# VectorE in the source's order in the experts' loop, with the gathered rows inside it; gates in column strips; the rows of f - m by way of DRAM; two weight loads ahead of the turn

## The chip, the cores and the metric

The kernel runs on one core of a Trainium2 chip. The metric is the device time of one execution in microseconds (us); smaller is better.

## The reference, cut to what matters

One decoder layer for 512 tokens (and 16 learned ones in front) of width 1024, in fp32. A diagonal state-space branch (S5) and a matrix-memory branch (mLSTM, four heads) are mixed by sigmoid gates; then each token picks 8 x 16 of 16384 single-neuron experts by product keys:

```python
y_s = s5_branch(u_s, ...) @ w_ssm_out          # ends in gelu, and a glu with w_glu
y_m = mlstm_branch(x_m, z_m, ...) @ w_ml_out
mixed = sigmoid(g_s) * y_s + sigmoid(g_m) * y_m
h = h + mixed @ w_out
...
gates = concatenate([q, k, v]) @ w_if + b_if   # mLSTM: log_i and log_f of each head
...
act = gelu(einsum('td,thkd->thk', xb, u_tab[eidx]))
out = einsum('thk,thkd->td', gate * act, v_tab[eidx])
```

## The kernel before, in words

`front` computes the branches and the mix, `peer` the experts. Products that need more than the fast fp32r format gives are done in three matmuls on a high and a low half (`mm3`, `proj`); `split` makes the halves: ScalarE copies the high half (L78), VectorE or GpSimd subtracts (L79). `wblock` (L156) loads a weight block through SP and splits it; two raw blocks and two pairs of halves exist at a time.

**Order.** The source is not the order of execution: a scheduler gives each engine and each queue its order from an estimated timeline, and the hardware then follows that order, each engine by itself. `keep_in_program_order` pins instructions of one engine against each other in the source's order; `later` and `after` only tell the scheduler that one thing comes after another.

**The turn (L560 to L583).** The S5 output ys lies with time in the partitions. Eight DMAs write it to yd in DRAM and eight read it back as yt, channels in the partitions, SP and ScalarE in turn. gsgate(4) and (5) stand behind it in the source, gsgate(6) and (7) after the gates (L650); gelu of yt, glu and so (w_ssm_out) follow.

**The gates (L550 to L605).** log_i and log_f of four heads, from xct and xmt (8 blocks of 128 channels each): each block is split, and the split weights wgt (100 columns wide, high and low halves in strips of their own) times high and low part give 64 matmuls into two accumulators. VectorE and ScalarE add up the strips into li and xf, and xf is transposed (xtp) for the log-sigmoid.

**Decay weights (L796).** `weights(h)` spreads head h's row of f - m (amu) over 128 partitions by a matmul with a selector (sel), then fourteen exponentials on ScalarE fill pm. It runs one head ahead of its use, at the top of the loop over heads.

**The experts' loop (L1401).** The first 128 tokens' experts are fetched row by row: `fetch` gathers 128 rows of u (or v) on GpSimd, `use` takes 128 dot products (u) or adds to ac0 (v) on VectorE; 231 of 256 rounds fall into this loop. The other 384 tokens go densely over 128 keys j: `hidden(j)` is 24 matmuls of 384 columns and a gelu, run six keys ahead (80 of the keys have been done before the loop, stored in ad and read back as acl); w(j) is that times the gates gin; v's block and w are split into vh, vl, wh, wl (three buffers each); `products` is 18 matmuls of 512 columns into op_. The last three keys' products run together, accumulator by accumulator, and the final norm follows (L1460). VectorE's order in the loop is the scheduler's, with hints (`pace`, `used`) that tie the uses to the products three keys back.

Of the kernel before, what the change touches and what calls it, by code (L numbers as in the profile page):

```python
# [18 lines left out]
OP = mybir.AluOpType  # L19
# [38 lines left out]
def f32(ap):  # L58
    return ap.bitcast(F32)
# [67 lines left out]
def front(tc, a, dbg, cst, dram, xnp, ident, h2d, gds, x0, qt01, dump, split, mm3, rsqrt, rsqrt_cols):  # L127
# [3 lines left out]
    with es:  # L131
# [78 lines left out]
        bif = small("bif", (H, 2), a["b_if"], A)  # L210
# [254 lines left out]
        later(tt(dsk, pv["ssm_d"].unsqueeze(2).to_broadcast([P, 4, CH]), m16.unsqueeze(1).to_broadcast([P, 4, CH]), OP.mult), xsc)  # L465
        gp_ = ptr("gk", (P, 4, P))
# [10 lines left out]
        def gsgate(b):  # L477
            hi, lo = wblock(a["w_in"][20 + b], f"wgs{b}")
# [71 lines left out]
        wgt = half("wgt", "pAr", (P, 16, 100), F32R)  # L550
        wg = [wgt[:, :8], wgt[:, 8:]]
        for j in range(2):
            GP.memset(f32(wg[j]), 0.0)
# [7 lines left out]
        for q in range(2):  # L561
# [26 lines left out]
        rwa = half("rwa", "pF")[:H]  # L588
        li, xf, e_, y_ = (rwa[:, n] for n in range(4))
        amu = small("amu", (H, T))  # L590
        gp = [ptr(f"gate{h}", (100, 264)) for h in range(2)]
        for k in range(16):
            if k % 2 == 0:
                xps = half(f"xp{k}", ("pAi", "pE")[k // 2 % 2], dt=F32R)
            xp = xps[:, k % 2 * 2:k % 2 * 2 + 2]
            split(xp[:, 0], xp[:, 1], (xct if k < 8 else xmt)[(k % 8) // 4][:, k % 4], (V, GP)[k % 2])
            for h in range(2):
                for n in range(2):
                    PE.matmul(gp[h], wg[k // 8][:, k % 8], xp[:, n, h * 264:(h + 1) * 264], start=k + n == 0, stop=k + n == 16)
        for h in range(2):  # L600
            c = slice(h * 264, (h + 1) * 264)
            A.activation(li[:, c], gp[h][64:64 + H], AF.Identity, bias=bif[:, 0:1])
            V.tensor_scalar(xf[:, c], gp[h][96:96 + H], bif[:, 1:2], None, op0=OP.add)
            tt(li[:, c], li[:, c], gp[h][0:H], OP.add)
            tt(xf[:, c], xf[:, c], gp[h][32:32 + H], OP.add)  # L605
# [8 lines left out]
        for n, c0 in enumerate(XC):  # L614
            PE.transpose(xtp[:, n], xf[:, c0:c0 + P], ident[:H, :H])
# [28 lines left out]
        tt(li, li, fl, OP.subtract)  # L644
        em = z_
# [121 lines left out]
        for h in range(H):  # L767
# [3 lines left out]
        sel = phase["q"].tile([H, H, P], F32, tag="sel", name="sel", bufs=1)  # L771
        GP.memset(sel, 1.0)
        GP.affine_select(sel, sel, pattern=[[-1, H], [0, P]], compare_op=OP.is_equal, fill=0.0, base=0,
                         channel_multiplier=1)
# [19 lines left out]
        pms = {}  # L794

        def weights(h):  # L796

            mup = pmm(f"mu{h}")
# [741 lines left out]
```

## Time and profile before

| | us |
|---|---|
| median of 3 runs | 1718.75 (1718.37 to 1719.97) |
| profiled execution, its own time | 1719.4 |
| its span, first to last instruction | 1717.5 |
| TensorE busy | 1665.9 |
| VectorE busy | 1316.3 |
| ScalarE busy | 710.2 |
| GpSimd busy | 715.0 |

The span is what the trace covers; the execution's own time has a little around it. Busy times of engines overlap. The granted clock is the share of TensorE's full clock (2.4 GHz) that it was given; it has two levels, 1.00 and 0.50.

### The profile page before, as it was taken

To read this page: it belongs to the slowest core of one execution; us is meant where nothing else is said; L and a number is where in the kernel's file an instruction comes from. 1 tells how busy PE (TensorE), PEld (TensorE's weight loads), DVE (VectorE), ACT (ScalarE), POOL (GpSimd) and SP (SyncE) were. 2 spreads that over 40 slices of the span, in tenths; PEclk is the share of its full clock that TensorE was granted. 3 is DMA by queue.
4 is the path that set the end of the run, shared out by engine and by line. 5 is a ranking of instruction groups with operands and counts; after the bars stand their busy time and mean duration, and the time that the engine had idled before them with its cause. 6 is when DMAs were issued, how large, how long until landed. Compare 5 with 4: busy or idle time off the path is not lost. (4 is left out here: it accounts for less than half of the span.)

```text
span 1717.5 us, 25552 instructions
## 1 busy us (share of the span) xinstructions
PE 1665.9 (97%) x9386; PEld 1470.0 (86%) x9386; DVE 1316.3 (77%) x2614; ACT 710.2 (41%) x1046; POOL 715.0 (42%) x486
## 2 busy tenths in 40 slices
PE   7998999999999999999999999999999998999996
PEld 6997788777888899999999988888888887888874
DVE  6996753366478899976874688787888787888897
ACT  4543635543332334456664334333333333333333
POOL 2022222223122378888884133333343334434570
PEclk9998999999999999999999999999999999999998
DMA  4514154112452346699999999999998999998994
GB/s 181 119 50 99 61 172 155 62 42 74 172 196 94 102 106 169 158 274 306 300 306 350 341 366 343 336 354 358 340 334 316 334 355 334 353 343 328 331 338 167
DMA packets 172773, 408.78 MB, mean 238 GB/s; under 512 B 44392, under 2 KB 89576, under 8 KB 171496
## 3 DMA queue, kind: packets, MB, share of 16 engines
q1 hardware_dynamic: 108816, 264.40, 44.0%
q0 software_dynamic: 55328, 134.31, 23.6%
q10 hardware_dynamic: 8504, 8.44, 1.7%
q8 instruction: 73, 1.20, 0.3%
q14 instruction: 52, 0.43, 0.1%
HBM read 359.81 MB, written 47.28 MB: 237 GB/s over the span
## 5 line engine op out<-in xcount | busy, mean ns | idle before, releaser
L82 PE MATMUL h<-x2h,uh 128*128 128x384 f32 x1024 | 346.0, 338 | 0.0
L85 PE MATMUL h<-x2l,uh 128*128 128x384 f32 x1024 | 343.6, 336 | 0.0
L86 PE MATMUL h<-x2h,ul 128*128 128x384 f32 x1024 | 343.6, 336 | 0.0
L85 PE MATMUL o<-vl,wh 128*128 128x512 f32 x768 | 303.6, 395 | 9.7 <-DVE vl L79 9.4
L86 PE MATMUL o<-vh,wl 128*128 128x512 f32 x768 | 301.1, 393 | 0.0
L82 PE MATMUL o<-vh,wh 128*128 128x512 f32 x768 | 267.5, 394 | 2.3 <-ACT vh L78 2.3
L1029 POOL DMA_INDIRECT g<-in_v,e x128 | 180.1, 1407 | 203.4 <-issue 80.0
L1252 POOL DMA_INDIRECT gds<-gw,ix x128 | 239.3, 1870 | 46.4 <-issue 37.2
L1029 POOL DMA_INDIRECT g<-in_u,e x103 | 125.4, 1218 | 246.8 <-DVE jk L1036 98.3
L78 ACT ACTIVATE wh<-w 128x384 fp32r<-128x384 f32 x128 | 67.1, 525 | 385.3 <-PE o L85 275.3
L78 ACT ACTIVATE uh<-u 128x1024 fp32r<-128x1024 f32 x128 | 135.9, 1062 | 202.3 <-PE h L85 182.2
L79 DVE TENSOR_TENSOR ul<-u,uh 128x1024 fp32r<-128x1024 f32 x128 | 156.2, 1220 | 70.0 <-ACT uh L78 69.5
L85 PEld LDWEIGHTS h<-x2l,uh 128*128 128x128 f32 x1024 | 192.3, 188 | 3.9
L82 PEld LDWEIGHTS h<-x2h,uh 128*128 128x128 f32 x1024 | 192.2, 188 | 3.5
L86 PEld LDWEIGHTS h<-x2h,ul 128*128 128x128 f32 x1024 | 192.2, 188 | 3.2
L85 PEld LDWEIGHTS o<-vl,wh 128*128 128x128 f32 x768 | 145.5, 189 | 43.6 <-DVE vl L79 14.9
L82 PEld LDWEIGHTS o<-vh,wh 128*128 128x128 f32 x768 | 144.5, 189 | 31.1 <-ACT vh L78 3.1
L86 PEld LDWEIGHTS o<-vh,wl 128*128 128x128 f32 x768 | 145.5, 189 | 28.2
L1043 DVE SCALAR_TENSOR_TENSOR ac<-g,w,ac 128x1024 f32<-128x1024 f32 x127 | 162.5, 1279 | 0.4
L79 DVE TENSOR_TENSOR vl<-v,vh 128x1024 fp32r<-128x1024 f32 x128 | 155.9, 1221 | 4.3 <-ACT vh L78 2.4
L79 DVE TENSOR_TENSOR wl<-w,wh 128x384 fp32r<-128x384 f32 x128 | 71.2, 557 | 94.5 <-ACT wh L78 92.2
L78 ACT ACTIVATE vh<-v 128x1024 fp32r<-128x1024 f32 x128 | 132.9, 1047 | 10.5 <-PE o L86 9.8
(541 smaller groups left out, 3050.2 us busy)
## 6 DMA issues: line engine op xcount, KB each, us to landing
u<-in_ut SPq DMA_DIRECT2D x128, 512.0 KB, 5.1
v<-in_v SPq DMA_DIRECT2D x128, 512.0 KB, 6.9
gd<-stg SPq DMA_DIRECT2D x8, 2048.0 KB, 7.5
gi<-gd SPq DMA_DIRECT2D x16, 1024.0 KB, 12.5
ad<-act SPq DMA_DIRECT2D x80, 192.0 KB, 3.4
acl<-ad SPq DMA_DIRECT2D x80, 192.0 KB, 6.8
gds<-qt SPq DMA_DIRECT2D x8, 1024.0 KB, 5.2
gi<-gds SPq DMA_DIRECT2D x16, 512.0 KB, 6.6
```

The lines of the kernel that those rows point to most:

```text
L78: A.activation(hi, src, AF.Copy)
L79: return eng.tensor_tensor(lo, src, f32(hi), op=OP.subtract)
L82: i_ = PE.matmul(ps, lh, rh, start=first, stop=False)
L85: PE.matmul(ps, lh, rl, start=False, stop=False)
L86: return PE.matmul(ps, ll, rh, start=False, stop=last)
L1029: return GP.indirect_dma_start(out=t, out_offset=None, in_=a["u"] if s_ < P else a["v"], in_offset=bass.IndirectOffsetOnAxis(ap=e0[:, c:c ...
L1043: i_ = V.scalar_tensor_tensor(ac0, g, w0[:, c:c + 1], ac0, op0=OP.mult, op1=OP.add)
L1252: i_ = GP.indirect_dma_start(out=gds.rearrange("b i j t -> (b i j t)").unsqueeze(1), out_offset=bass.IndirectOffsetOnAxis(ap=ix[:, c:c + 1 ...
```

## The change

- **Turn.** All sixteen DMAs go through SP. gsgate(4) stands ahead of the turn in the source, and so do the loads and splits of the weights for gsgate(5) and (6); gsgate(5) to (7) run after the gates.
- **Gates.** No splits and no halves: wgt is plain fp32, 32 columns for each block; four blocks run in four column strips of the array, each into its own 32 partitions of the accumulator, 32 matmuls in all. The four strips are added by a matmul with sel8 (1 where the partition is head row n of its strip), which also turns xf into xtp; li comes from a second such product. The bias is one column over the partitions.
- **Rows of f - m.** amu is stored to DRAM (mud), and each head's row is read back by a broadcast DMA into SBUF. `weights(h + 1)` stands after the squares of head h in the source; the exponentials of heads 2 and 3 come after the squares two heads back.
- **Experts' loop.** From its start all of VectorE's work is pinned in source order: the low half of u's block, w, the low half of v's block, one use, the low half of w, the other uses of this key. The hints for gathers and uses are gone.

```diff
-        bif = small("bif", (H, 2), a["b_if"], A)
+        bif = small("bif", (P, 1))
+        GP.memset(bif, 0.0)
+        for n in range(2):
+            A.dma_start(bif[H * n:H * (n + 1)], a["b_if"][:, n:n + 1])
...
+        sel8 = small("sel8", (P, 2 * H))
+        later(V.tensor_reduce(sel8, ident.rearrange("p (k c) -> p c k", c=2 * H), axis=AX.X, op=OP.add), xsc)
...
-        wgt = half("wgt", "pAr", (P, 16, 100), F32R)
-        wg = [wgt[:, :8], wgt[:, 8:]]
...
+        wgt = half("wgt", "pAr", (P, 16, 32))
+        GP.memset(wgt, 0.0)
         for b, n in ((0, 0), (8, 2)):
-            for g in range(2):
-                split(wg[b // 8][:, :, 32 * g:32 * g + 4], wg[b // 8][:, :, 64 + 32 * g:68 + 32 * g], wgs[:, n, :, 4 * g:4 * g + 4])
+            V.tensor_copy(wgt[:, b:b + 8, :2 * H], wgs[:, n])
...
+        mix.append(half("mix1", "mix1", (P, 4, S)))
+        gsgate(4)
+        wg56 = [wblock(a["w_in"][20 + b], f"wgs{b}") for b in (5, 6)]
...
         for t_ in range(L):
-            (SY, A)[t_ % 2].dma_start(yd[t_].rearrange("g c n -> c g n"), ys[t_ * CH:(t_ + 1) * CH])
+            SY.dma_start(yd[t_].rearrange("g c n -> c g n"), ys[t_ * CH:(t_ + 1) * CH])
         for t_ in range(L):
-            (SY, A)[t_ % 2].dma_start(yt[:, :, t_], yd[t_].rearrange("(q g) c n -> (g c) q n", q=4))
-        mix.append(half("mix1", "mix1", (P, 4, S)))
-        for b in range(4, 6):
-            gsgate(b)
+            SY.dma_start(yt[:, :, t_], yd[t_].rearrange("(q g) c n -> (g c) q n", q=4))
...
-            split(xp[:, 0], xp[:, 1], (xct if k < 8 else xmt)[(k % 8) // 4][:, k % 4], (V, GP)[k % 2])
...
+        for k in range(0, 16, 4):
+            xk = (xct if k < 8 else xmt)[k % 8 // 4]
             for h in range(2):
-                for n in range(2):
-                    PE.matmul(gp[h], wg[k // 8][:, k % 8], xp[:, n, h * 264:(h + 1) * 264], start=k + n == 0, stop=k + n == 16)
+                for r in range(4):
+                    i_ = PE.matmul(gp[h][32 * r:32 * r + 32], wgt[:, k + r], xk[:, r, h * 264:(h + 1) * 264],
+                                   start=k == 0, stop=k == 12)
+                    if r:
+                        tc.keep_in_program_order(i_)
...
         for h in range(2):
...
+            A.activation(gsum[:, h * 264:(h + 1) * 264], gp[h], AF.Identity, bias=bif)
...
-            PE.transpose(xtp[:, n], xf[:, c0:c0 + P], ident[:H, :H])
+            PE.matmul(xtp[:, n], gsum[:, c0:c0 + P], sel8[:, H:], start=True, stop=True)
+        for h in range(2):
+            PE.matmul(lip[h], sel8[:, :H], gsum[:, h * 264:(h + 1) * 264], start=True, stop=True)
+            A.copy(li[:, h * 264:(h + 1) * 264], lip[h])
...
+        SY.dma_start(mud, amu[:, NM:])
...
-        for b in range(6, NK):
-            gsgate(b)
+        for b in range(5, NK):
+            gsgate(b, wg56.pop(0) if wg56 else None)
...
-            mup = pmm(f"mu{h}")
-            PE.matmul(mup, sel[:, h], amu[:, NM:], start=True, stop=True)
+            mup = phase["q"].tile([P, S], F32, tag="mu", name=f"mu{h}", bufs=2)
+            SY.dma_start(mup, mud[h:h + 1].to_broadcast([P, S]))
...
+                for i_ in turn_ if h > 1 else ():
+                    later(i_, squares[h - 2])
...
-                weights(h + 1)
                 gmgate(2 * h)
...
+            if h + 1 < H:
+                weights(h + 1)
             rs = rsqrt_cols(sm, hss, NT, "hn")
...
+        def inorder(ins):
+            if loop[0]:
+                tc.keep_in_program_order(ins)
+            return ins
...
-            split(hi, lo, raw, eng)
+            inorder(split(hi, lo, raw, eng))
...
+        loop[0] = True
         for j in range(NKEY):
...
+            inorder(V.tensor_tensor(w.rearrange("p (b t) -> p b t", t=TB), gin[:, :, j % JB],
+                                    acts.pop(j).rearrange("p (b t) -> p b t", t=TB), op=OP.mult))
...
+            A.activation(wh, w, AF.Copy)
...
-            low = split(vh, vl, raw)
-
-            if j >= 5:
-                after(low, used[j - 5])
...
+            inorder(split(vh, vl, raw))
+
+            upto = min(j + 1, NKEY - 6) * (2 * P - NEARLY) // (NKEY - 6)
+            for last in (0, 1):
+                while due < (upto if last else min(due + 1, upto)):
+                    n = NEARLY + due
+                    due += 1
+                    fetch(n, vp.tile([P, D], F32, tag="gt", name=f"g{n}", bufs=7))
+                    inorder(use(n, vp.tile([P, D], BF16, tag="jk", name=f"jk{n}", bufs=1)))
+                    if not last:
+                        break
+                if not last:
+                    inorder(V.tensor_tensor(wl, w, f32(wh), op=OP.subtract))
...
-            while due < min(j + 1, NKEY - 6) * (2 * P - NEARLY) // (NKEY - 6):
-                n = NEARLY + due
-                due += 1
-                after(fetch(n, vp.tile([P, D], F32, tag="gt", name=f"g{n}", bufs=7)), pace[j - PACE - 2] if j >= PACE + 2 else None)
-                last_use = use(n, vp.tile([P, D], BF16, tag="jk", name=f"jk{n}", bufs=1))
-                after(last_use, pace[j - PACE] if j >= PACE else None)
```

## Rows read from the trace of the kernel before

**Rows 1.** The head of the profile's page: the span, and for each engine its busy time, its share of the span and its instructions.
```profile
span 1717.5 us, 25552 instructions
...
PE 1665.9 (97%) x9386; PEld 1470.0 (86%) x9386; DVE 1316.3 (77%) x2614; ACT 710.2 (41%) x1046; POOL 715.0 (42%) x486
```
**Rows 2.** The table of stretches of 43 us: the stretch, its length, then busy time and instructions of PE, PEld, DVE, ACT and POOL, the granted clock of TensorE, the busy share of the DMA engines and GB/s.
```profile
129.00:172.00 43.00, 35.73 (x292) 31.68 (x291) 27.79 (x37) 17.05 (x24) 8.99 (x5) 0.89 0.42 101
...
1419.00:1462.00 43.00, 38.05 (x170) 32.36 (x169) 34.78 (x38) 12.24 (x17) 19.73 (x15) 0.92 0.91 335
```
**Rows 3.** The waits of TensorE over the whole span: who waited for whom, us in total, times, the longest.
```profile
PE gs L82 <- ACT wgs_h L78: 6.1, 1, 6.1
...
PE gs L86 <- POOL wgs_l L79: 1.2, 1, 1.2
...
PE o L85 <- DVE vl L79: 9.4, 6, 4.9
```
**Rows 4.** ScalarE's part of the timeline around the turn (start, length, instruction, in brackets the idle time before it and what ended it), and one row of the table of stretches of 2 us (columns as in rows 2).
```profile
160.29 4.72 ACTq L583 DMA_DIRECT2D yt<-yd  x4
...
165.14 1.06 ACT L78 ACTIVATE wgs_h<-wgs_w 128x1024 fp32r<-128x1024 f32 x1 [9.30 <-DMA yt<-yd]
...
169.16 1.28 ACT L654 ACT_TABLE_LOAD   x1 [1.50 <-DMA yt<-yd]
...
160.00:162.00 2.00, 0.20 (x2) 0.00 (x0) 0.00 (x0) 0.00 (x0) 0.00 (x0) 1.00 0.95 185
```
**Rows 5.** The table of stretches, cut where the granted clock changes (columns as in rows 2).
```profile
166.25:172.49 6.24, 5.02 (x11) 3.52 (x12) 2.02 (x1) 4.71 (x5) 2.36 (x1) 0.50 0.70 179
...
1444.42:1449.08 4.66, 4.66 (x11) 3.69 (x12) 4.53 (x4) 0.00 (x0) 2.62 (x2) 0.50 0.93 347
```
**Rows 6.** TensorE's part of the timeline, two product matmuls of 512 columns with ten between them.
```profile
1668.09 0.39 PE L85 MATMUL o<-vl,wh 128*128 128x512 f32 x1
...
1670.59 0.39 PE L86 MATMUL o<-vh,wl 128*128 128x512 f32 x1
```
**Rows 7.** TensorE's part of the timeline: the first and the last run of gk (eight runs of eight records; a plain fp32 matmul leaves two records), sixteen of the 64 gate matmuls, and the two plain fp32 matmuls of the first head's queries.
```profile
96.76 0.43 PE L472 MATMUL gk<-w1r,gk 128*32 128x128 f32 x8
...
98.31 0.40 PE L472 MATMUL gk<-w1i,gk 128*32 128x128 f32 x8
...
158.10 2.10 PE L599 MATMUL gate<-xp,wgt 128*100 128x264 f32 x16
...
246.81 1.88 PE L738 MATMUL q<-xct,bdq 128*128 128x512 f32 x4
```
**Rows 8.** The first head's sel product in the timeline, and from the groups by line and form the transposes into xtp (busy us, mean ns of one, idle time before).
```profile
248.62 1.12 PE L799 MATMUL mu<-amu,sel 4*128 4x512 f32 x2
...
L615 PE MATMUL xtp<-ident,rwa 4*128 4x4 f32 x5 | 0.6, 206 | 0.0
```
**Rows 9.** The timeline of VectorE and of TensorE around the longest wait for vl.
```profile
1438.67 0.56 DVE L79 TENSOR_TENSOR wl<-w,wh 128x384 fp32r<-128x384 f32 x1 [5.44 <-ACT wh L78]
...
1443.14 2.35 DVE L79 TENSOR_TENSOR vl<-v,vh 128x1024 fp32r<-128x1024 f32 x2
...
1444.42 0.79 PE L85 MATMUL o<-vl,wh 128*128 128x512 f32 x1 [4.95 <-DVE vl L79]
```
**Rows 10.** Groups by line and form in the stretch from 920 to 1700 us: busy us, mean ns of one, idle time before the group and what ended it.
```profile
L79 DVE TENSOR_TENSOR vl<-v,vh 128x1024 fp32r<-128x1024 f32 x128 | 155.9, 1221 | 4.3 <-ACT vh L78 2.4
...
L79 DVE TENSOR_TENSOR wl<-w,wh 128x384 fp32r<-128x384 f32 x128 | 71.2, 557 | 94.5 <-ACT wh L78 92.2 <-PE h L86 1.6
...
L79 DVE TENSOR_TENSOR ul<-u,uh 128x1024 fp32r<-128x1024 f32 x55 | 67.3, 1223 | 36.5 <-ACT uh L78 36.3
...
L978 DVE TENSOR_TENSOR w<-gi,acl 128x384 f32<-128x384 f32 x80 | 44.4, 555 | 3.6 <-DMA acl<-ad 2.3
...
L1043 DVE SCALAR_TENSOR_TENSOR ac<-g,w,ac 128x1024 f32<-128x1024 f32 x127 | 162.5, 1279 | 0.4
...
L78 ACT ACTIVATE vh<-v 128x1024 fp32r<-128x1024 f32 x128 | 132.9, 1047 | 10.5 <-PE o L86 9.8 <-DMA v<-in_v 0.7
```
**Rows 11.** The timeline at the start of the experts' loop: SP, VectorE and TensorE (the two h matmuls have seventeen between them).
```profile
958.29 4.77 SPq L1414 DMA_DIRECT2D v<-in_v  x1
...
962.46 1.23 DVE L79 TENSOR_TENSOR ul<-u,uh 128x1024 fp32r<-128x1024 f32 x1 [2.02 <-ACT uh L78]
...
967.83 1.23 DVE L79 TENSOR_TENSOR ul<-u,uh 128x1024 fp32r<-128x1024 f32 x1 [1.74 <-ACT uh L78]
...
972.49 0.56 DVE L978 TENSOR_TENSOR w<-gi,acl 128x384 f32<-128x384 f32 x1 [2.29 <-DMA acl<-ad]
...
974.29 0.33 PE L82 MATMUL h<-x2h,uh 128*128 128x384 f32 x1
...
977.41 0.33 PE L82 MATMUL h<-x2h,uh 128*128 128x384 f32 x1
```
**Rows 12.** The timeline of the tail: TensorE, then VectorE.
```profile
1673.19 0.50 PE L85 MATMUL o<-vl,wh 128*128 128x512 f32 x1 [1.53 <-DVE vl L79]
...
1686.86 0.49 PE L82 MATMUL o<-vh,wh 128*128 128x512 f32 x1 [0.71 <-ACT vh L78]
...
1687.83 1.23 DVE L79 TENSOR_TENSOR vl<-v,vh 128x1024 fp32r<-128x1024 f32 x1
...
1698.00 0.69 DVE L1464 TENSOR_TENSOR hr<-o,hr 128x512 f32<-128x512 f32 x1 [2.83 <-PE o L86]
```

More of the change, by code (lines that the diff above doesn't have):

```diff
@@ L475, in front, with gsgate @@
         mix = [half("mix0", "mix0", (P, 4, S))]
-        def gsgate(b):
-            hi, lo = wblock(a["w_in"][20 + b], f"wgs{b}")
+        def gsgate(b, w=None):
+            hi, lo = w or wblock(a["w_in"][20 + b], f"wgs{b}")
             p = pmm(f"gs{b}")
@@ L580, in front @@
         for t_ in range(L):
-            (SY, A)[t_ % 2].dma_start(yd[t_].rearrange("g c n -> c g n"), ys[t_ * CH:(t_ + 1) * CH])
+            SY.dma_start(yd[t_].rearrange("g c n -> c g n"), ys[t_ * CH:(t_ + 1) * CH])
         for t_ in range(L):
-            (SY, A)[t_ % 2].dma_start(yt[:, :, t_], yd[t_].rearrange("(q g) c n -> (g c) q n", q=4))
-        mix.append(half("mix1", "mix1", (P, 4, S)))
-        for b in range(4, 6):
-            gsgate(b)
-        rwa = half("rwa", "pF")[:H]
+            SY.dma_start(yt[:, :, t_], yd[t_].rearrange("(q g) c n -> (g c) q n", q=4))
+        rwf = half("rwa", "pF")
+        rwa = rwf[:H]
         li, xf, e_, y_ = (rwa[:, n] for n in range(4))
         amu = small("amu", (H, T))
[L591 to L595, printed above, removed]
-            split(xp[:, 0], xp[:, 1], (xct if k < 8 else xmt)[(k % 8) // 4][:, k % 4], (V, GP)[k % 2])
-            for h in range(2):
-                for n in range(2):
-                    PE.matmul(gp[h], wg[k // 8][:, k % 8], xp[:, n, h * 264:(h + 1) * 264], start=k + n == 0, stop=k + n == 16)
-        for h in range(2):
[L601 to L605, printed above, removed]
+        gp = [ptr(f"gate{h}", (P, 264)) for h in range(2)]
+        for k in range(0, 16, 4):
+            xk = (xct if k < 8 else xmt)[k % 8 // 4]
+            for h in range(2):
+                for r in range(4):
[3 more added lines that the diff above has]
+                        tc.keep_in_program_order(i_)
+        gsum = rwf[:, 3]
+        for h in range(2):
+            A.activation(gsum[:, h * 264:(h + 1) * 264], gp[h], AF.Identity, bias=bif)
+        lip = [ptr(f"lip{h}", (H, 264)) for h in range(2)]
         rwb = half("rwb", "pE")
@@ L770, in front @@
         queries(0)
[L771 to L774, printed above, removed]
         cmask = small("cmask", (P, P))
@@ L793, in front @@
         OFF = [0, 512, 896, 1152]
-        pms = {}
+        pms, squares = {}, []
         def weights(h):
-            mup = pmm(f"mu{h}")
-            PE.matmul(mup, sel[:, h], amu[:, NM:], start=True, stop=True)
+            mup = phase["q"].tile([P, S], F32, tag="mu", name=f"mu{h}", bufs=2)
+            SY.dma_start(mup, mud[h:h + 1].to_broadcast([P, S]))
             pm = half(f"pm{h}", "pm", (P, 1408))
@@ L808, in weights @@
                         tt(o, mu, cmask, OP.add)
-                    A.activation(o, o if i == j else mu, AF.Exp, bias=cb[:, slot(j, i), h:h + 1])
+                    turn_.append(A.activation(o, o if i == j else mu, AF.Exp, bias=cb[:, slot(j, i), h:h + 1]))
+                for i_ in turn_ if h > 1 else ():
+                    later(i_, squares[h - 2])
             pms[h] = pm
@@ L987, in peer @@
         acts = {}
+        loop = [False]
+        def inorder(ins):
+            if loop[0]:
+                tc.keep_in_program_order(ins)
+            return ins
         clock = [0.0]
@@ L1398, in products @@
             return last
-        due, used = 0, []
+        due = 0
+        loop[0] = True
         for j in range(NKEY):
```

21 lines of the change are left out of this document (8 added, 13 removed).

## The prediction

> **What bounds the kernel now.** The share of busy time comes first: TensorE is busy for 1665.9 of 1717.5 us [rows 1], so the change can only win where TensorE waits, where it runs at 1.2 instead of 2.4 GHz, or where it is given less to do. The table of stretches shows where the first two are: a 43 us stretch at 129 us in which it is busy 35.7 us at a granted clock of 0.89, and one at 1419 us with 38.0 us at 0.92 [rows 2]. TensorE's own waits give the names: 6.1 and 1.2 us for the gate weights wgs ahead of the gs products, and 9.4 us in six pieces for vl in the experts' loop [rows 3]. Everything else on VectorE, ScalarE and the queues lies beside TensorE's work, so work taken off them counts only through these waits.
>
> **The change part by part.** The sum is made against the profiled execution, 1719.4 us.
>
> **1. The turn (rows through yd and yt) and gs.** ScalarE issues half of the turn's DMAs; its last four hold it from 160.29 to 165.01, and only then does it split the weights of gs6 [rows 4]. That is the 6.05 us wait; the 1.22 us wait for the low half follows from it. After it the clock is at half until 172.49, and TensorE's 5.02 us of work there would have been 2.5 at full clock [rows 5]. Together 9.8 us. In the new kernel ScalarE issues none of these DMAs, the weights of gs5 and gs6 are asked for ahead of the turn, and SP issues all sixteen; behind them on SP stand the loads for gs7 and glu. What is late next is yt itself, for glu. From 158.1, where TensorE starts on the gates, it has the gates (3.9, below), gs6 and gs7 (24 matmuls each at 0.227 [rows 6], 10.9 together): until 172.9. yt had landed at 169.2 [rows 4]; the table load (1.3), then the gelu and the first splits (3.2, an estimate as three instructions like the split of 1.06 us [rows 4]) put glu at 173.7. So 0.8 us, say 1, of new wait if the turn keeps its length. Four issues took ScalarE 4.72 us beside as many on SP; sixteen in a row at that rate take 18.9 instead of half of that, so the other end is 9.4 us more, which eats the gain. Against that end: during the turn the DMA engines were 95% busy [rows 4], so the issue times look like back-pressure and not like work of the issuer. I take a **gain of 8.8**, with 0 to 9.8 as ends.
> The Trainium skill, "DMA: Bandwidth & Descriptors", section "Issuing engines are not separate DMA queues", says that DMAs from several engines share the same 16 DMA engines and that using more issuers saves only issue time. By that rule the turn keeps its length; by the issue times alone it doubles. No run here shows the turn on one queue.
>
> **2. The gates in column strips.** Before, 64 matmuls on split operands; sixteen of them take 2.10 us [rows 7], all 8.4. After, 32 plain fp32 matmuls of 128x32 by 264 columns, four strips at a time. The nearest row is gk, the same form with 128 columns: from 96.76 to 98.71 for 32 of them [rows 7], 0.24 per group of four. Two plain 128x512 matmuls take 1.88 us, so 1.84 ns a column; a group of four strips with 128 columns at that rate is 0.235, so four strips run in the time of one. Eight groups of 264 columns: 8 x 264 x 1.84 ns = 3.9 us. If they ran one after the other it would be 15.5; the gk rows speak for 3.9. **Gain 4.5**, ends 4.5 and -7.1. ScalarE, VectorE and GpSimd lose 16, 8 and 8 splits; VectorE so ends the conv, which the gates wait for, a little sooner. New on TensorE: five products with sel8 in place of five transposes (0.6 us for these, five records of 206 ns [rows 8]; I take 0.8) and two of 264 columns for li (2 x 264 x 1.84 ns = 1.0). **Cost 1.2**, 0 to 2. bif by a memset and two small DMAs, the sel8 reduction (one small VectorE instruction), and the copy into wgt are covered by the loads and products around them; without cover they are under 1 us.
>
> **3. Rows of f - m through DRAM.** One sel product takes 1.12 us and there are four [rows 8]: **gain 4.5**. The row now comes by a broadcast DMA on SP. If its load has to wait (two buffers, so the third waits for the first head's exponentials) the w_z and gm loads behind it wait too. A head's TensorE work covers this (gm alone is 24 x 0.227 = 5.5 us); without cover it costs the DMA's latency per head. weights(h+1) stands later in the source but is tied only to the squares two heads back, so I cost the move at nothing; ends 0 and +4, if the last head, which has no z products ahead of it, waits for its exponentials.
>
> **4. Experts' loop, the middle.** At 1438.67 VectorE does a wl, then two uses, a w and an ul, and vl only at 1443.14; TensorE waits 4.95 us to 1444.42 [rows 9] and has half clock for its next 4.66 us of work [rows 5], 2.3 lost. In the new order vl(j) comes directly after w(j). **Gain 7.3.** Whether the fixed order brings new waits: per key VectorE needs 1.22 (vl), 0.56 (wl), 0.56 (w) and 1.89 uses at 1.28, so 4.8 us, and 1.22 more with an ul; TensorE needs 18 x 0.227 = 4.1, and 24 x 0.173 = 4.15 more with a hidden block (18 of its matmuls from 974.29 to 977.41) [rows 6, 10, 11]. In eight keys, three of them with a hidden block, that is 42 against 45 us: VectorE keeps up, but narrowly. vl(j) can start when products(j-3) has freed its buffers and ScalarE has split v (1.05); through vl, one use and wl it takes 4.1 to 4.6 us, while products(j-2) and (j-1) last 8.2. So 3.6 us of lead: no waits in the steady state, as long as each load and gathered row is there when VectorE's turn comes.
>
> **5. The loop's start.** Here the order costs. Before the first product TensorE has hidden blocks; counted in order, the ul's at 962.46 and 967.83 are those of keys 9 and 11, done ahead of w(0), which waits for acl until 972.49 [rows 11]. In the new order they stand behind w(2) and w(4). TensorE so runs out of hidden blocks 2 x 4.15 us earlier, at 969.6 instead of 977.9. With w(0) where it was, its first product starts at 973.5 and the last third of them, after vl, a use and wl, at 976: 4 to 5 us idle and 2 to 3 of half clock. But SP stood 4.77 us on the load of v(4), ahead of acl, and v(4) needs vl(0), which now comes after w(0): acl has to go first, and may be there at 972.5 - 4.8 = 967.7. I take a **cost of 3**, ends 0 and 8.
>
> **6. The tail.** By key 121 all uses are done in source order, where VectorE now still mixes them among the last vl. That ends the wait of 1.53 us until 1673.19 [rows 12]. Let T be the end of products(124), 1686.15, from where TensorE waits 0.71 [rows 12]. The last three keys' products start with a vl that a use delayed (1687.83), and the first add on a finished accumulator waits until 1698.00, T + 11.9; from there to the end it is VectorE's chain, 19.5 us. New: vh, vl and wl of key 127 until T + 3.5, the chain of the first 128 rows (5, an estimate from the 19.5 for three such chains and the last store; now pinned behind them), then the 19.5 us: T + 28.0 instead of T + 31.4. **Gain 1.5 + 3.4 = 4.9**, ends 1.5 and 9.
>
> **Sum:** 8.8 + 4.5 - 1.2 + 4.5 + 7.3 - 3 + 4.9 = 25.8. 1719.4 - 25.8 = 1693.6; the median before lies 0.65 below the profiled run, so **1693 us**.
>
> **The rivals.** (a) One queue makes the turn longer: glu waits up to 9.4 us more, 1693 + 9 = **1702**. For it: the issue times; against it: the busy DMA engines. (b) The loop's start costs its upper end, or the gates' or last head's exponentials wait: 1693 + 6 = **1699**. (c) Slower: VectorE's fixed order meets late data. If a gathered row or an acl is late at the head of its queue, vl, wl and the next uses all stand behind it, and TensorE pays what it paid at 1439: 5 us of wait and 2.3 of clock. The DMA engines are 91% busy in the stretch at 1419 us [rows 2], and a VectorE with 42 of 45 us of work wins back only 3 us in eight keys. Four such stops (29 us) use up the gain, five give 1693 + 36 = **1729**. Against it: in the loop before, no wait of TensorE goes back to a gather, and seven row buffers at 1.9 uses a key reach 3.7 keys ahead. (d) Everything lands at its good end (3 less at the start, 4 less in the tail): **1686**. (e) The strips don't run side by side: 1693 + 11.6 = **1705**.
> For (e) the Trainium skill, "TensorEngine Tiling (Array Packing)", section "Key Properties", says that tiles work independently but that a change of tiling mode drains TensorE. The gk rows agree on the first, and whatever drain there is lies inside their 1.95 us.
>
> **How the numbers follow.** Forecast 0.50 (1688 to 1698), (a) 0.12, (b) 0.12, (c) 0.11, (d) 0.11, (e) 0.04. What a measurement can tell from no change is 0.2%, 3.4 us. Of (c), 0.03 fall within that and 0.08 beyond; where (a), (b) or (e) come together with stops of (c) I add 0.02 to each side: same 0.05, slower 0.10, faster 0.85. The range leaves out half of (d) and nearly all of (c): 1684 to 1712.
>
> **What would show it.** The turn: no DMA issue on ScalarE between 147 and 175, no wait ahead of gs; a wait ahead of glu instead is (a). The gates: one run of some 4 us. No mu matmuls. The loop: no wait of TensorE for vl between its start and key 121; a wait right before the first o product is step 5, and VectorE waiting for a DMA ahead of w or a use is (c). The forecast is wrong above all if the order that the scheduler gives TensorE and ScalarE in the first 500 us changes for other reasons: then waits stand there that none of these steps names.

## The result, and the profile after

The changed kernel takes **1698.4 us** (median of 1696.09, 1698.37 and 1699.87; the kernel before 1718.6 beside it), a ratio of 0.988 with a 95% interval of 0.986 to 0.990. A fourth run, at 1918.13 us with a mean granted clock of 0.80, was disturbed and is left out. The forecast was 1693 with a range of 1684 to 1712. So the sign and the range held and the size was 5 us off; but the sum was right for partly wrong reasons. The profiled execution (1696.09 us, span 1694.4) shows it stage by stage, cut at the first matmul of z (the z gates of the mLSTM heads), of mo (w_ml_out) and of sc (the experts' scores), and at T, the end of products(124). Counted in order, 18 matmuls a key, the first matmul behind products(124) starts at 1685.31 before and at 1666.23 after:

| stretch | before, us | after, us | gain | forecast |
|---|---|---|---|---|
| start to z (steps 1, 2) | 223.7 | 220.3 | 3.4 | 8.8 + 4.5 - 1.2 = 12.1 |
| z to mo (step 3) | 161.4 | 158.6 | 2.8 | 4.5 |
| mo to sc | 113.1 | 113.0 | 0.1 | 0 |
| sc to T (steps 4, 5, part of 6) | 1187.1 | 1174.3 | 12.8 | 7.3 - 3 + 1.5 = 5.8 |
| T to the end (step 6) | 32.2 | 28.2 | 4.0 | 3.4 |
| sum | 1717.5 | 1694.4 | 23.1 | 25.8 |

TensorE's timeline at T, before and then after:

```profile
1685.31 0.39 PE L82 MATMUL o<-vh,wh 128*128 128x512 f32 x1
...
1666.23 0.39 PE L82 MATMUL o<-vh,wh 128*128 128x512 f32 x1
```

Ahead of mo the change gave 10 us less than forecast, from sc to the end 8 us more. Of the 3.4 us ahead of z, about 1.5 are no part of the change: the trace before has half clock from 25.7 to 29.1 us and the one after has not, and xm begins at 43.43 and at 41.95. A run with the new front and half clock there (e2_front_only, below) starts z at 221.30, 2.4 ahead of the kernel before. The stretch in the trace before (columns as in [rows 2]):

```profile
25.70:29.10 3.40, 3.40 (x17) 3.40 (x17) 1.62 (x10) 0.00 (x0) 0.00 (x0) 0.50 0.28 113
```

The head of the page, for [rows 1]:

```profile
span 1694.4 us, 25464 instructions
...
PE 1650.4 (97%) x9387; PEld 1461.3 (86%) x9387; DVE 1279.9 (76%) x2599; ACT 690.6 (41%) x1021; POOL 709.3 (42%) x476
```

TensorE's waits after the change, for [rows 3] (us in total, times, the longest):

```profile
PE xm L346 <- DVE xmt L181: 2.2, 1, 2.2
PE gs L82 <- ACT wgs_h L78: 2.0, 1, 2.0
...
PE v L769 <- DVE vm L763: 1.5, 1, 1.5
...
PE o L85 <- DVE vl L79: 0.8, 1, 0.8
```

The six waits for vl, 9.4 us before [rows 3], are down to one of 0.8, behind T. But three waits of 1.5 to 2.2 us stand there that no step named: for xm (the mLSTM branch's input), for gs and for v (its values); the ones of 11.2 us for u and 2.0 for x2t are about as long before. At each of them another engine does something else ahead of what TensorE needs. First xm, the timeline of VectorE, then TensorE:

```profile
121.60 0.44 DVE L181 TENSOR_TENSOR xmt<-xm,nt 128x264 f32<-128x264 f32 x1
121.94 4.84 DVE L443 SCALAR_TENSOR_TENSOR xct<-xmt,par,xct 128x527 f32<-128x527 f32 x7
126.69 0.44 DVE L181 TENSOR_TENSOR xmt<-xm,nt 128x264 f32<-128x264 f32 x1
...
127.18 0.39 PE L346 MATMUL xm<-xnh,wx_h 128*128 128x264 f32 x1 [2.18 <-DVE xmt L181]
```

VectorE does seven convs before it copies a finished xm out of its accumulator, and TensorE waits 2.18 us for that accumulator. A smaller wait of the same kind stands earlier: for w1r, behind an addition of the mix on VectorE, 1.10 us where the kernel before waits 0.24.

```profile
72.87 1.97 PE L455 MATMUL l1p<-ident,w1r 128*128 128x128 f32 x16 [1.10 <-DVE w1r L181]
```

Then the turn (the timeline of SP, ScalarE, TensorE), for [rows 4]:

```profile
152.08 7.63 SPq L586 DMA_DIRECT2D yd<-ys  x8
159.81 4.92 SPq L588 DMA_DIRECT2D yt<-yd  x8
...
156.49 1.06 ACT L78 ACTIVATE wgs_h<-wgs_w 128x1024 fp32r<-128x1024 f32 x1 [4.43 <-issue]
...
167.31 1.28 ACT L661 ACT_TABLE_LOAD   x1 [6.42 <-DMA yt<-yd]
168.60 1.92 ACT L661 ACTIVATE yg<-yt 128x2048 f32<-128x2048 f32 x1
170.55 2.20 ACT L78 ACTIVATE ygh<-yg 128x512 fp32r<-128x512 f32 x4
...
174.86 1.04 ACT L78 ACTIVATE wgs_h<-wgs_w 128x1024 fp32r<-128x1024 f32 x1
...
175.95 0.79 PE L82 MATMUL gs<-xnh,wgs_h 128*128 128x512 f32 x1 [2.05 <-ACT wgs_h L78]
```

ScalarE issues nothing of the turn any more, and gs6's split is done by 157.6. But ScalarE's next split, gs7's, stands behind the gelu (with its splits and some small work for the gates), and the gelu waits for the rows until 167.31. That puts gs7 at 175.95, where the forecast had gs7 done by 172.9. The turn takes 15.2 us from first issue to gelu; it took 13.3. Third, v: the pm row is VectorE's mask addition on the row of f - m, which waited 1.85 us for its DMA, ahead of the copy that v needs. SP had issued the store of amu at 187.19 and issued the load of the first row only at 231.03, behind loads of weights.

```profile
238.52 0.90 DVE L181 TENSOR_TENSOR pm<-mu,cmask 128x128 f32<-128x128 f32 x4 [1.85 <-DMA mu<-mud]
239.34 0.42 DVE L763 COPY vm<-vm 128x256 f32<-128x256 f32 x1
...
239.81 0.71 PE L769 MATMUL v<-bdv,xmt 128*128 128x128 f32 x4 [1.49 <-DVE vm L763]
```

The gates, for [rows 7], are one run of 3.77 us where the forecast had 3.9:

```profile
156.56 1.99 PE L599 MATMUL gate<-xct,wgt 128*32 128x264 f32 x32
158.37 1.96 PE L599 MATMUL gate<-xmt,wgt 128*32 128x264 f32 x32
```

The loop, VectorE's timeline at its start and near the old wait of 4.95 us [rows 9, 11], then TensorE's first product:

```profile
963.68 0.56 DVE L1431 TENSOR_TENSOR w<-gi,acl 128x384 f32<-128x384 f32 x1 [10.20 <-DMA acl<-ad]
...
1432.09 0.55 DVE L1431 TENSOR_TENSOR w<-gi,acl 128x384 f32<-128x384 f32 x1
1432.56 1.22 DVE L79 TENSOR_TENSOR vl<-v,vh 128x1024 fp32r<-128x1024 f32 x1
1433.70 1.28 DVE L1058 SCALAR_TENSOR_TENSOR ac<-g,w,ac 128x1024 f32<-128x1024 f32 x1
1436.84 0.56 DVE L1450 TENSOR_TENSOR wl<-w,wh 128x384 fp32r<-128x384 f32 x1 [1.87 <-ACT wh L1435]
...
964.85 0.97 PE L82 MATMUL o<-vh,wh 128*128 128x512 f32 x3 [0.20 <-ACT wh L1435]
```

w, vl, use, wl, as the change says, with VectorE idle 1.87 us ahead of wl: it keeps up. The tail's VectorE, for [rows 12]:

```profile
1667.76 1.23 DVE L79 TENSOR_TENSOR vl<-v,vh 128x1024 fp32r<-128x1024 f32 x1 [1.92 <-ACT vh L78]
...
1669.38 0.69 DVE L1482 TENSOR_TENSOR hr<-ac,hr 128x512 f32<-128x512 f32 x1
...
1674.57 0.68 DVE L1482 TENSOR_TENSOR hr<-o,hr 128x512 f32<-128x512 f32 x1
```

wl of key 127 ends at T + 3.2, the chain of the first 128 rows takes 5.2, and 19.8 more lead to the end: T + 28.2, where the forecast had 3.5 + 5 + 19.5 = 28.0.

**The clock has a part of its own.** The table of stretches, cut where the clock changes, for [rows 5]:

```profile
128.19:135.02 6.83, 6.83 (x34) 6.83 (x33) 6.83 (x8) 1.40 (x2) 2.81 (x1) 0.50 0.50 155
...
175.98:179.39 3.41, 3.29 (x7) 2.20 (x8) 3.10 (x14) 2.79 (x3) 0.00 (x0) 0.50 0.30 36
```

Half clock follows each of the two new waits of 2 us. To compare kernels I split each run's time into what half clock took, as an estimate (1 - mean granted clock) x time, and the rest; the clock is given to 0.001, so a mean over the runs is good to about 1 us. The estimate is too high as it stands, since it counts half clock also where TensorE waits or is done: in the tail, where TensorE has no work left, that is half of 9 us before and of 9.7 after. Only its differences between kernels are read. The tail, before and after:

```profile
1708.50:1717.50 9.00, 0.00 (x0) 0.00 (x0) 4.63 (x15) 2.44 (x6) 0.00 (x0) 0.50 0.32 117
...
1684.66:1694.40 9.74, 0.00 (x0) 0.00 (x0) 5.04 (x16) 2.85 (x6) 0.00 (x0) 0.50 0.29 108
```

Before: 19 and 1699 us; after: 14.2 and 1684.0. So by this estimate 15 us of the gain are waits and work, and 5 are clock.

### The profile page after: what moved, and what is told of

The parts are those of the page before. It is cut to its first block, busy times and chain, and to the rows that moved or that the text cites. A ratio compares the mean times of both kernels' runs of the same rounds, so it can differ in the third digit from the quotient of the medians.

```text
span 1694.4 us, 25464 instructions
## 1 busy us (share of the span) xinstructions
PE 1650.4 (97%) x9387; PEld 1461.3 (86%) x9387; DVE 1279.9 (76%) x2599; ACT 690.6 (41%) x1021; POOL 709.3 (42%) x476
## 4 chain that ended last, share of the span: by engine, by line
PE 84%; DVE 8%; DMA 4%; ACT 2%; issue 2%; POOL 0%; SPq 0%; ACTq 0%; DVEq 0%; POOLq 0%
PE h L82 10%; PE h L85 10%; PE h L86 10%; PE o L82 10%; PE o L86 10%; PE o L85 10%; PE gp L1333 2%; PE q L86 2%; PE q L85 2%; PE q L82 2%; DMA wo<-in_w_out 1%; PE s L839 1%; PE n L848 1%; PE gm L346 1%; PE gm L349 1%
## 5 line engine op out<-in xcount | busy, mean ns | idle before, releaser
L85 PE MATMUL o<-vl,wh 128*128 128x512 f32 x768 | 280.1, 391 | 0.8 <-DVE vl L79 0.8
L82 PE MATMUL o<-vh,wh 128*128 128x512 f32 x768 | 280.3, 391 | 0.2 <-ACT wh L1435 0.2
L1043 POOL DMA_INDIRECT g<-in_v,e x128 | 200.2, 1564 | 187.7 <-DVE ac L1058 169.1
L86 PE MATMUL o<-vh,wl 128*128 128x512 f32 x768 | 266.5, 390 | 0.5 <-DVE wl L1450 0.5
L1043 POOL DMA_INDIRECT g<-in_u,e x103 | 115.6, 1122 | 217.3 <-DVE jk L1050 214.3
L1024 ACT ACTIVATE act<-h 128x384 f32<-128x384 f32 x128 | 61.6, 481 | 224.3 <-PE h L86 224.2
L1050 DVE SCALAR_TENSOR_TENSOR jk<-g,x 128x1024 bf16<-128x1024 f32 x103 | 125.5, 1219 | 0.0
```

The lines of the kernel that those rows point to most:

```text
L82: i_ = PE.matmul(ps, lh, rh, start=first, stop=False)
L85: PE.matmul(ps, lh, rl, start=False, stop=False)
L86: return PE.matmul(ps, ll, rh, start=False, stop=last)
L1024: A.activation(acts[j], p, AF.Gelu_apprx_tanh)
L1043: return GP.indirect_dma_start(out=t, out_offset=None, in_=a["u"] if s_ < P else a["v"], in_offset=bass.IndirectOffsetOnAxis(ap=e0[:, c:c ...
L1050: i_ = V.scalar_tensor_tensor(jk, g, 1.0, x0, op0=OP.mult, op1=OP.mult, accum_out=hsl[:, c:c + 1])
```

## The experiments

Theory: the loop is worth about 17 us; the front's gain is mostly given back by two new waits of TensorE, for xm's copy and for gs7's split, that come from the order on VectorE and ScalarE. Rivals: the turn on one queue is itself the loss; or each step is worth what was costed and the difference lies elsewhere. Medians of 3 to 6 runs, each kernel beside the kernel before on the same chip (1717.6 to 1719.0 there); the last column is of the mean of the runs:

| run | us | ratio to before, 95% | half clock, rest |
|---|---|---|---|
| changed kernel | 1698.4 | 0.986 to 0.990 | 14.2, 1684.0 |
| e1_loop_only | 1702.5 | 0.989 to 0.992 | 13.6, 1688.4 |
| e2_front_only | 1712.3 | 0.995 to 0.998 | 17.5, 1694.7 |
| e3_turn_two_queues | 1691.8 | 0.983 to 0.986 | 10.6, 1681.6 |
| e4_gs7_first | 1690.3 | 0.983 to 0.986 | 10.1, 1680.8 |
| e5_convs_later | 1696.3 | 0.986 to 0.989 | 14.8, 1681.2 |
| e6_both | 1691.3 | 0.983 to 0.985 | 9.1, 1681.2 |
| e7_gates_before | 1700.7 | 0.988 to 0.991 | 12.3, 1688.2 |
| e8_rows_by_pe | 1706.1 | 0.991 to 0.993 | 14.2, 1690.8 |
| e9_uses_free | 1700.0 | 0.988 to 0.991 | 14.9, 1685.4 |
| e10_strips_serial | 1705.5 | 0.991 to 0.994 | 12.3, 1692.2 |
| e11_convs_tied | 1687.1 | 0.980 to 0.983 | 7.1, 1680.3 |
| e12_tied_two_queues | 1692.9 | 0.984 to 0.986 | 10.5, 1682.3 |

**e1_loop_only and e2_front_only: which half.** Each has one half of the change: everything ahead of the experts' half, or that half. A line or two of each diff against the changed kernel stands for the rest, e1's first.

```diff
-            SY.dma_start(yd[t_].rearrange("g c n -> c g n"), ys[t_ * CH:(t_ + 1) * CH])
+            (SY, A)[t_ % 2].dma_start(yd[t_].rearrange("g c n -> c g n"), ys[t_ * CH:(t_ + 1) * CH])
...
```

```diff
-            inorder(split(vh, vl, raw))
+            low = split(vh, vl, raw)
...
```

> The experts' half is that of the changed kernel (steps 4 to 6), all before it that of the kernel before (steps 1 to 3 undone). Theory A (front mostly given back): the changed kernel's loop and tail are worth what the comparison of the two traces shows between the start of the scores and the end, 13.6 to the last product group plus 3.2 behind it, so 17 us: 1701 to 1703 us, and the scores start at 498 us as in the kernel before. Theory B (each step is worth what the prediction said and the difference in the loop comes from elsewhere, such as the clock or the queues that the front leaves behind): 7.3 - 3 + 4.9 = 9 us, so 1709 to 1710 us.

> The other half: steps 1 to 3 as changed, the experts' loop and tail of the kernel before. Theory A: the front gains the 6.2 us that the scores start earlier in the changed kernel's trace, and the loop has its old waits for vl again: 1711 to 1713 us. Theory B: 8.8 + 4.5 - 1.2 + 4.5 = 16.6 us, so 1702 us. If the two halves' gains don't add up to that of the changed kernel (19), the loop's gain depends on what the front leaves behind.

Measured 1702.5 and 1712.3: 15.1 and 5.2 us less than the kernel before beside them, 20.3 together where the changed kernel has 20. Theory A on both, and the halves add up. From the first score to the end e1 takes 1202.5 us, the changed kernel 1202.4, the kernel before 1219.3. In e2 the waits for vl are all back, to the tenth:

```profile
PE o L85 <- DVE vl L79: 9.4, 6, 5.0
```

**e4_gs7_first: the order on ScalarE.**

In the function that loads and splits a weight block, phase["low"] keeps the last low half so far, which is gs7's where the gelu is written; a low half needs ScalarE's part of the split first.

```diff
+            phase["low"] = i_
...
-        A.activation(yg, yt.rearrange("p q l n -> p q (l n)"), AF.Gelu_apprx_tanh)
+        later(A.activation(yg, yt.rearrange("p q l n -> p q (l n)"), AF.Gelu_apprx_tanh), phase["low"])
```

> The changed kernel with the gelu on the rows of y tied behind ScalarE's part of the split for gs7. Theory A (the wait of 2.05 us ahead of gs7 is there because ScalarE's order has the gelu, which waits for the rows of y until 167.3 us, ahead of that split): the wait goes, and with it the 1.7 us that the half clock behind it cost: 1695 to 1696 us, if nothing at glu takes its place. Rival (glu is now the bound: it needs the gelu and its splits, which come about 2 us later): the wait moves to glu and the time stays at 1698 to 1700 us.

Measured 1690.3, 8 us better and not 3. The wait is gone and glu starts at 178.44 and not at 184.01. ScalarE's timeline: the split, then the gelu's table load, at 170.22, without a wait for the rows.

```profile
167.21 1.06 ACT L78 ACTIVATE wgs_h<-wgs_w 128x1024 fp32r<-128x1024 f32 x1
...
170.22 1.28 ACT L662 ACT_TABLE_LOAD   x1
```

Why more than the 2.05 us of the wait: in the changed kernel's profiled execution TensorE came late to that wait, since the half clock at 128 us had slowed it. e8, with the same front and no half clock there, has a wait of 5.1 us at the same place, and gs7 starts at 175.82 there and at 175.95 in the changed kernel. So the bound was the chain of rows, gelu and split, and the half clock ahead of it cost nothing. e8's TensorE:

```profile
175.82 0.79 PE L82 MATMUL gs<-xnh,wgs_h 128*128 128x512 f32 x1 [5.09 <-ACT wgs_h L78]
```

By the table, 3.2 us of e4's gain are waits and 4.1 clock.

**e3_turn_two_queues: one queue or two.**

```diff
-            SY.dma_start(yd[t_].rearrange("g c n -> c g n"), ys[t_ * CH:(t_ + 1) * CH])
+            (SY, A)[t_ % 2].dma_start(yd[t_].rearrange("g c n -> c g n"), ys[t_ * CH:(t_ + 1) * CH])
...
-            SY.dma_start(yt[:, :, t_], yd[t_].rearrange("(q g) c n -> (g c) q n", q=4))
+            (SY, A)[t_ % 2].dma_start(yt[:, :, t_], yd[t_].rearrange("(q g) c n -> (g c) q n", q=4))
```

> The changed kernel with the turn's sixteen DMAs issued alternately by SP and ScalarE again, as before; gs5 and gs6 keep their weights loaded ahead. Theory A (the turn's length is set by the DMA engines, and its place on ScalarE only held the splits up): the rows of y land no more than 2 us earlier after the first of them is issued, ScalarE is held until the last issue, so the splits ahead of gs6 come late again and the time is 1701 to 1706 us. Rival (one queue is itself the loss, since glu's and gs7's work starts when the rows have landed): the rows land 5 us or more earlier, the new wait ahead of gs7 goes, and the time falls to 1694 to 1696 us.

Measured 1691.8: faster, as the rival had it and by more than it said, though the rows come only 2 us sooner, as theory A had it (13.1 us from the first issue, 152.60, to the gelu's table load, 165.73). The wait ahead of gs7 stays (2.26 us), but it ends 1.6 us sooner (174.37). Where the rows bound gs7, two queues do help; how much of the 6.6 us they do can't be read off: 2.4 are waits and work, the rest clock.

**e5_convs_later and e6_both: the convs' order in the source.**

```diff
-        for b in range(4):
-            conv(b, turned)
         for b in range(4, NK):
             xmproj(b)
-            conv(b, turned)
+            conv(b - 4, turned)
+        for b in range(4, NK):
+            conv(b, turned)
```

> The changed kernel with VectorE's convs of blocks 0 to 3 put, in the source, one behind each of the copies of xm blocks 4 to 7, and those of 4 to 7 behind them, so that no copy of xm out of its accumulator stands behind seven convs. Theory A (TensorE's wait of 2.18 us at 125 us for the copy of xm comes from VectorE's order alone): the wait goes, and in the executions in which half clock follows it 1.7 to 3.4 us more: 1694 to 1697 us. Rival (the convs are needed as early as they are, for the products that end in y and for the gates): the wait comes back as one ahead of y or of the gates, and the time is 1698 to 1702 us.

> The two edits together: gs7's split ahead of the gelu, and the convs behind the copies of xm. The first alone gave 1690.3 us. Theory A (the two waits are independent, each with its own half clock): 2.2 to 4 us less than that, 1686 to 1688 us, and no wait of TensorE above 1 us between 72 and 230 us. Rival (once one of them is gone, the rows of y that glu needs are the bound of the stage): a wait of about 2 us ahead of glu, and 1690 us.

Neither tested what it was made for. In both, VectorE still does the seven convs (4.84 us) ahead of the copy, and TensorE waits 2.17 and 2.19 us: the order in the source does not decide here, the scheduler's does. The intervals of e5 and the changed kernel overlap, and e6 repeats e4.

**e11_convs_tied: the same by a tie.** On top of e4:

```diff
-        for b in range(4):
-            conv(b, turned)
-        for b in range(4, NK):
-            xmproj(b)
-            conv(b, turned)
+        copied = [xmproj(b) for b in (4, 5)]
+        for b in range(6):
+            conv(b, copied[1])
+        for b in range(6, NK):
+            conv(b, xmproj(b))
```

> The run with gs7's split first, and with all convs tied behind the second copy of xm block 5, so that the wait of 2.18 us at 125 us must go (the source order alone had not moved it). Theory A (after gs7's split is out of the way that wait is on the path again): 2 us less than with the split alone, 1688 to 1689 us, and more in executions in which half clock followed it. Rival (the rows of y through the turn are the next bound, and glu waits for what is won): the wait appears ahead of glu, and 1690 us.

Measured 1687.1, the best of all, 11.3 us below the changed kernel. Both copies of xm come ahead of the convs (VectorE's timeline), and TensorE's wait for them is gone; 0.36 us for a low half of wx's weights are left there:

```profile
121.73 0.78 DVE L182 TENSOR_TENSOR xmt<-xm,nt 128x264 f32<-128x264 f32 x2
...
122.55 3.48 DVE L444 SCALAR_TENSOR_TENSOR xct<-xmt,par,xct 128x527 f32<-128x527 f32 x5
```

By the table the gain over e4 is 0.5 us of waits and 3.0 of clock, so little of it is the wait itself: in the profiled execution no half clock stands ahead of 1676.9. Part of the rival is there as well: glu now waits 0.51 and 0.26 us for its weights' split.

**e12_tied_two_queues: the queues, without the other bound.** e11 with e3's edit.

> The run before this one, with the turn's DMAs on two queues again, which landed the rows of y some 2 us sooner after the first issue in an earlier run. Theory A (what remains ahead of glu is TensorE's own work): the same time as the run before this one, within 1 us, or 1 us more where ScalarE's issues hold up a split. Rival (the turn's length is the bound of the stage by then): 1.5 to 2 us less than the run before this one.

Measured 1692.9, 5.9 us worse than e11. Neither expectation had the size; what the prediction's step 1 said of ScalarE's issues is what happens. The timeline of ScalarE, then TensorE:

```profile
157.98 3.78 ACTq L589 DMA_DIRECT2D yt<-yd  x3
161.88 1.06 ACT L78 ACTIVATE wgs_h<-wgs_w 128x1024 fp32r<-128x1024 f32 x1 [8.50 <-DMA yt<-yd]
...
163.36 0.83 ACT L607 ACTIVATE rwa<-gate,bif 128x264 f32<-128x264 f32 x2
...
163.88 2.30 PE L618 MATMUL xtp<-sel,rwa 128*128 128x4 f32 x10 [3.19 <-ACT rwa L607]
```

ScalarE is held by its issues until 161.8 and then does a split and a mix, so the gates leave their accumulator late and TensorE waits 3.19 us, with half clock behind it. With the gelu behind gs7's split, one queue was faster; with the gelu ahead of it (e3), two were.

**e7_gates_before: step 2 undone.**

```diff
-                    i_ = PE.matmul(gp[h][32 * r:32 * r + 32], wgt[:, k + r], xk[:, r, h * 264:(h + 1) * 264],
-                                   start=k == 0, stop=k == 12)
+                    PE.matmul(gp[h], wg[k // 8][:, k % 8], xp[:, n, h * 264:(h + 1) * 264], start=k + n == 0, stop=k + n == 16)
...
```

> The changed kernel with step 2 undone: the gates from split operands in 64 matmuls, the five transposes, no sel8 products, no bias in 16 rows. Theory A (step 2 is worth what the prediction said, and the two new waits come from other parts): 4.5 - 1.2 = 3.3 us more, so 1702 to 1703 us, with both waits still there. Rival (the splits that step 2 takes off VectorE are what let seven convs go ahead of the copy of xm, and the sel8 products' results on ScalarE are what stands ahead of gs7's split, so that step 2 pays for its own gain): one or both waits go, and the time is 1695 to 1699 us.

Measured 1700.7, between the two, and 2.3 above the changed kernel (the intervals overlap); by the table 4.2 more in waits and work, and 1.9 less of clock. Half of the rival holds: the 2.18 us for xm's copy are gone (0.93 and 0.44 us for wx_l stand in its place, 0.95 and 0.46 in the kernel before), so step 2 did turn that order over (that the splits it takes off VectorE do it is likely, and not shown by itself), and the wait for w1r is back at 0.24. The other half falls: gs7's split stands behind the gelu without any sel8 product, and the wait is longer. ScalarE, then TensorE:

```profile
168.63 1.28 ACT L656 ACT_TABLE_LOAD   x1 [10.93 <-DMA yt<-yd]
...
173.96 1.04 ACT L78 ACTIVATE wgs_h<-wgs_w 128x1024 fp32r<-128x1024 f32 x1
...
175.05 0.79 PE L82 MATMUL gs<-xnh,wgs_h 128*128 128x512 f32 x1 [8.27 <-ACT wgs_h L78]
```

So that order is not step 2's. It stands in e2 too, without the new loop, and in e8, without the rows through DRAM: it belongs to step 1.

**e10_strips_serial: do strips run side by side.**

```diff
-                    i_ = PE.matmul(gp[h][32 * r:32 * r + 32], wgt[:, k + r], xk[:, r, h * 264:(h + 1) * 264],
-                                   start=k == 0, stop=k == 12)
+                    i_ = PE.matmul(gp[h], wgt[:, k + r], xk[:, r, h * 264:(h + 1) * 264],
+                                   start=k + r == 0, stop=k + r == 15)
```

> The changed kernel with all 32 gate matmuls in one strip of 32 columns, summed by one accumulator, so that none can lie beside another. At 1.84 ns a column they take 32 x 264 x 1.84 ns = 15.5 us and not 3.8. Theory A (the stretch ahead of gs7 is bound by the rows of y, which reach ScalarE at 167.3 us, and its split for gs7 that stands behind them until 175.9 us, so that TensorE's work there is partly covered): 15.5 - 3.8 less the wait of 2.05 us and the 1.7 us of clock behind it, 8 to 10 us more, 1707 to 1709 us, and no wait ahead of gs7. Rival (nothing covers it): 11.7 us more, 1711 us. That four strips don't run side by side, against the changed kernel's own trace, would give no difference.

Measured 1705.5, 7.1 more; z starts 8.4 us later and nothing waits for gs7. Theory A in its mechanism, a little below its time (the rest of the table is 8.2 more). The gates take 14.4 us (157.89 to 172.31) for 3.77:

```profile
157.89 7.31 PE L599 MATMUL gate<-xct,wgt 128*32 128x264 f32 x32
165.03 7.28 PE L599 MATMUL gate<-xmt,wgt 128*32 128x264 f32 x32
```

**e8_rows_by_pe: step 3 undone, the place of the weights kept.**

```diff
-            mup = phase["q"].tile([P, S], F32, tag="mu", name=f"mu{h}", bufs=2)
-            SY.dma_start(mup, mud[h:h + 1].to_broadcast([P, S]))
+            mup = pmm(f"mu{h}")
+            PE.matmul(mup, sel[:, h], amu[:, NM:], start=True, stop=True)
```

> The changed kernel with step 3 undone: the rows of f - m by a sel product on TensorE, 1.12 us each, four of them, and not through DRAM; the weights stay where the change put them. Theory A (the sel products were plain extra work of TensorE): 4.5 us more, 1703 to 1704 us. Rival (half of it comes back, since the stage from z to mo took 2.8 us less in the changed kernel and not 4.5, a new wait of 1.5 us for v at 238 us being part of that): 2 to 3 us more, 1701 to 1702 us, and the wait at 238 us is gone.

Measured 1706.1, 7.8 more, above both. The 1.5 us wait for v is gone, as the rival said, but the last head waits for its weights (TensorE's waits):

```profile
PE s L841 <- DVE pm L842: 2.3, 1, 2.3
...
PE n L850 <- DVE pm L842: 1.6, 1, 1.6
```

4 x 1.12 + 2.3 + 1.6 - 1.5 = 6.9, and the rest (without clock) is 6.8 us above the changed kernel's. So this isn't step 3 alone. The last head's sel product runs at 358.34 here, where the changed kernel asks for that head's row at 249.39: the late place of the weights is covered only while their rows come from DRAM. What step 3 alone is worth was not run.

**e9_uses_free: what ends the waits for vl.**

```diff
-                    fetch(n, vp.tile([P, D], F32, tag="gt", name=f"g{n}", bufs=7))
-                    inorder(use(n, vp.tile([P, D], BF16, tag="jk", name=f"jk{n}", bufs=1)))
+                    after(fetch(n, vp.tile([P, D], F32, tag="gt", name=f"g{n}", bufs=7)), pace[j - 5] if j >= 5 else None)
+                    after(use(n, vp.tile([P, D], BF16, tag="jk", name=f"jk{n}", bufs=1)), pace[j - 3] if j >= 3 else None)
```

> The changed kernel with the uses of the gathered rows (and the gathers themselves) taken out of VectorE's fixed order in the loop and given the hints of the kernel before; ul, w, wl and vl stay fixed, vl behind w. Theory A (what ends the waits for vl is that vl stands right behind w, whatever the uses do): no wait for vl between the loop's start and key 120, and 1697 to 1701 us. Rival (the uses in their place are what does it: left free, they crowd in front of a vl as in the kernel before): waits for vl again, the one of 5 us with its 2.3 us of half clock at least, and 1705 us or more.

Measured 1700.0: theory A. No wait for vl in the loop. The fixed uses matter only at its start: here w(0) runs at 967.03 (behind a load of u, by the trace) and not at 963.68, and TensorE waits 3.34 us, with 3.4 us at half clock around it.

```profile
968.20 1.22 PE L82 MATMUL o<-vh,wh 128*128 128x512 f32 x2 [3.34 <-ACT wh L1434]
```

## Why the prediction was right or wrong

**Step 1 failed,** at the sentence "it has the gates (3.9, below), gs6 and gs7 ...: until 172.9". It took for granted that gs7's split runs when ScalarE is free. ScalarE runs what it is given in the given order; the split was placed behind an instruction that waits for the rows, and gs7 began at 175.95 (in e8 at 175.82, with TensorE idle for 5.09 us before it). The old form of the wait (a split behind issues that wait for DMA engines) was taken away, and a new form (a split behind a gelu that waits for the same rows) took its place, with half clock again. e4 shows it. That the wait would come at glu was the wrong place; the prediction's last sentence, that the scheduler's order in the first 500 us is what could upset it, was right, but no chance and no price stood beside it.

**The turn's length,** rival (a), was mis-sized only: 1.9 us of up to 9.4. The Trainium skill, "DMA: Bandwidth & Descriptors", section "Issuing engines are not separate DMA queues", has several issuers save issue time and nothing more; 15.2 against 13.3 us, and 13.1 in e3 on two queues, is near that and far from the doubling by issue times alone.

**Step 2** was right in its parts: 3.77 us for the gates, and e10's 14.4 us show that the strips do run side by side, which ends rival (e). What it left out: VectorE's order changed with it, the convs moved ahead of xm's copy and an addition ahead of w1r (0.9 us more of wait). e7 puts the whole step at about 2 us, or 4 without the clock, where the sum had 3.3; that lies within what these runs can tell.

**Step 3** gave 2.8 of 4.5. "I cost the move at nothing" failed for the first head: its row was asked for at 231.03, landed at 238.5 and held VectorE up, ahead of the copy for v (1.49 us). In e3, e5 and e9 that wait is not there, since half clock shortly before it slows TensorE, and z to mo takes 158.6 to 158.7 all the same.

**Step 4** was right in its mechanism (e1, e9) and too small. Counting each matmul's step beyond 0.173 us (h) and 0.227 us (o), keys 61 to 90, with the wait of 4.95 in them, give 8.9 us (9.8 to 0.9) where 7.3 was costed; keys 3 to 60 and 91 to 113 give 2.8 more, in stalls mostly too short to be listed as waits, for which the prediction had no term; keys 114 to 124 give 2.7 where step 6 had 1.5. What each of those short stalls waited for stays open.

**Step 5:** acl did go first, w(0) ran at 963.68, and the cost was 1.6 us (0.8 before the first product and 0.8 in keys 0 to 2), not 3; half clock did not come in the profiled execution.

**Step 6** was right in its new chain: T + 28.2 for T + 28.0. Its reading of T before was late: by 1686.15 the first three matmuls of key 125 were done, and products(124) ended at 1685.31, so the old tail was T + 32.2 and the gain 4.0, not 3.4. Rival (c) did not occur: no use or w in the middle of the loop held TensorE up.

So 10 us too much ahead of mo and 8 too little from sc on nearly cancelled, which is luck: by e1 and e2 the halves add up, so neither error made the other. e11, with the two orders mended, starts z at 213.7, 10.0 us ahead of the kernel before (1.5 of them the half clock at 26 us), where steps 1 and 2 had forecast 12.1.

## What to carry to other kernels

When a wait is taken off an engine that runs its instructions in a fixed order, list what else on it waits for the same event and what stands behind it: the wait may only change its name. Work taken off one engine lets a scheduler reorder it, so tie the few instructions that free an accumulator or feed TensorE, and check in the trace that the tie, not the source order, moved them. A stage bound by one chain hides losses ahead of it: half clock ahead of gs7 changed nothing while the rows bound it (e8). So mend the bound first, and then what stands ahead of it; the tie of the convs was run only on top of e4.

## What the runs showed of the hardware

The granted clock differs from run to run of one kernel. Nine traces (the changed kernel, e2 to e6, e8, e9 and e10) have the same wait of 2.2 us at about 125 us; in six of them 6.8 us at half clock follow, in e3, e4 and e8 none. Over the runs of the changed kernel the mean clock is 0.991 to 0.993, over those of e11 0.995 to 0.997. By the table e11 is 7.1 us ahead of the changed kernel through the clock and 3.7 through waits: taking two waits of 2 us away was worth more through the clock than by themselves. Not all of it is theirs. Of the half clock ahead of the tail in the changed kernel's trace, 10.2 us stand behind these two waits and 3.4 at 381 us, where e11 changes nothing and yet has none.
